# Issue order planned from other operation costs, LayerNorm squares on ScalarE, and a norm's squares summed on VectorE

## Chip, cores and metric

The kernel runs on one core of one Trainium2 chip. The metric is the device time of one execution in microseconds (us). The core's engines are TensorE (PE in the rows, its weight loads PEld), VectorE (DVE, V in the code), ScalarE (ACT, S), GpSimd (POOL, G) and SyncE (SP, Q), which issues nearly all DMA transfers.

## What is computed

One block of an encoder on 512 tokens with 1024 channels, all in float32. `rms_norm` divides by the root of the mean square over the channels.

```python
x = x + 0.5 * swiglu_ffn(rms_norm(x, ffn1_norm[l]), ffn1_w13[l], ffn1_w2[l])
h = rms_norm(x, mix_norm[l])
proj = h @ w_in[l]
a, g, q, k, v, fl = jnp.split(proj, splits, axis=-1)
y_conv = conv_module(a, g, conv_w[l], conv_b[l], conv_ln_g[l], conv_ln_b[l])
y_attn = forgetting_attention(q, k, v, fl + forget_b[l])
y = jnp.concatenate([rms_norm(y_conv, out_norm_conv[l]),
                     rms_norm(y_attn, out_norm_attn[l])], axis=-1)
x = x + y @ w_out[l]
x = x + 0.5 * swiglu_ffn(rms_norm(x, ffn2_norm[l]), ffn2_w13[l], ffn2_w2[l])
...
return rms_norm(x, final_norm)
```

`conv_module` is a gated input, a causal depthwise convolution of 31 taps over 512 channels, LayerNorm over those channels, and silu. `forgetting_attention` is causal softmax attention of 8 heads of 64, with a bias from a running sum of log-sigmoid gates. Each half-step (`swiglu_ffn`) has 2816 hidden channels.

## The kernel before

Channels lie on the 128 partitions and the 512 tokens along the free axis, so x is 8 tiles of 128x512. A product of full precision is made from three passes: each operand is split into a high part in the reduced format fp32r and a low rest, and high·high, high·low and low·high are summed in one PSUM bank. So a product over 1024 channels is 24 matmuls of 512 columns. The activations' parts are `xh` and `xl`. A weight tile (`raw`, 512 KB by DMA) gets its high part `whi` by a ScalarE copy and its low part `wlo` by a VectorE subtraction; each has two buffers (`SPLITS`), which are taken in the order of the weight units: `whi81` for the first attention pair's q, `whi82` for its k, `whi83` and `whi84` for the second pair's, up to `whi88`, then `whi89` for the output projection.

The stages are: the first half-step (products `f1g`, `f1u`, `f1p`, `f1o`); the input projection, which gives the convolution's gate and value (`pg`, `pa`), values and gates of attention (`pv`), and q and k of four pairs of heads (`pq`, `pk`); convolution and attention beside these; the output projection (`wo`, part 0 from the convolution's channels, part 1 from the attention's); and the second half-step (`f2g`, `f2u`, `f2p`, `f2o`) with the final norm.

The four tiles of the convolution (`conv_tile`) are summed tap by tap: tiles 1 and 3 on VectorE (`conv`), tiles 0 and 2 by a ScalarE product per tap (`tap`, two buffers) and a GpSimd addition (`acc`). Attention (`attention`) goes per pair of heads, block of 128 queries and head: scores `s` on PE into one of two banks, a VectorE instruction that adds the gate's bias and takes the minimum (`sm`, `mn`), an exponential on ScalarE, a transposition on PE (`pt`, one bank), a ScalarE copy (`pT`), and the product with the values (`po`). `pt5_0` and `s5_3` are such steps of head 5, blocks 0 and 3.

After the last tap LayerNorm is made in `conv_norm`: the mean by a PE sum over the partitions (`ssq_mean`) that is spread back (`rb_mean`), VectorE subtracts it from the four tiles, GpSimd squares them (`sq_ln`), PE sums the squares (`ssq_ln`), ScalarE takes the root (`rc_ln`), VectorE the reciprocal, PE spreads it (`rb_ln`), ScalarE copies it (`rstd_ln`), and then the tiles are scaled, put through silu and split into `yh` and `yl`. Their squares (`sq_conv`) go to PE for a further norm (`ssq_conv`, `rb_conv`).

The class `Stats` sums squares in one of two ways: `pair` gives two squared tiles at a time to PE, and `add` has VectorE add each square to an accumulator, which PE sums once, in `rstd`. For the second half-step's norm (`f2in`) the kernel before uses `pair` in `w_out`, part 1. The first `f2g` product doesn't need that norm; its result is scaled by `rstd_f2in` when it leaves PSUM. Products share three PSUM banks (`mm`).

ScalarE holds one table of functions at a time. Root, sigmoid, exponential and silu each ask for an `ACT_TABLE_LOAD` if another table is loaded.

The order of all instructions is set by `Plan`. The code records operations with their engine and the tiles that they read and write; `price` gives each a cost, and `schedule` places them one by one: the operation that can start earliest on its engine, and among those the one with the highest rank, which is the longest path of costs behind it plus an urgency (`URGENT...`, given where it is recorded). A change of the ScalarE table costs 1.3 in this plan and lowers the rank by 40. All recorded instructions show as line 240 in the profile, so the rows are told apart by tile names.

Of the kernel before, what the change touches and what calls it, by code (L numbers as in the profile page):

```python
# [36 lines left out]
P = 128  # L37
T = 512
D = 1024
KD = D // P  # L40
# [33 lines left out]
SEM = 0.15  # L74
COPY, ACT = 0.05, 0.07
PENALTY = 40.0
URGENT_IN, URGENT_STATS, URGENT_V, URGENT_LF, URGENT_LN, URGENT_END = 20.0, 200.0, 200.0, 200.0, 200.0, 200.0
URGENT_Q, URGENT_OUT, URGENT, URGENT_X = 3.0, 3.0, 50.0, 50.0

# [65 lines left out]
class Buf:  # L145
    def __init__(self, make, dt, slots):
        self.make, self.dt, self.slots, self.tile = make, dt, slots, None
        self.uses, self.left = [], 0

# [15 lines left out]
class Plan:  # L165
# [5 lines left out]
    def __init__(self, tc):  # L171
        self.tc, self.ops, self.tags, self.joined, self.urgency = tc, [], {}, None, 0.0

    def tile(self, pool, shape, dt, tag, name, bufs=1):
        slots = self.tags.setdefault((id(pool), tag), Slots(bufs))
        buf = Buf(lambda: pool.tile(shape, dt, tag=tag, name=name, bufs=bufs), dt, slots)
        slots.queue.append(buf)
        size = int(np.prod(shape))
        if View._bytes.size < size:
# [64 lines left out]
    def price(self, engine, method, args, kwargs, out):  # L244

        n = out.n if isinstance(out, View) else 512
        if engine == "PE":
            dt = args[1].buf.dt
            passes = 4 if dt == F32 and method == "matmul" else 2 if dt == F32 else 1
            part = args[1].at[0].size / P if method == "matmul" else 1  # L250
            return 0.003 + n * passes / 2400.0 * max(part, 0.25), None
        if method == "dma_start" and engine != "Q":
            return 0.1, None
        if engine == "S":
            if method == "copy":
                return COPY + n * 0.00084, None
            return ACT + n * 0.00084, None if args[2] in (AF.Copy, AF.Square, AF.Identity) else args[2]
        if engine == "G":
            return 0.1 + n * (0.0024 if method.startswith("tensor_") else 0.0012), None
        if engine == "Q":  # L260
            return 0.1 + n * 4 * P / 330e3, None
        if method == "tensor_tensor_scan":
            return 0.06 + n * 0.0022, None
        if method == "reciprocal":
            return 0.06 + n * 0.0064, None
        if method == "scalar_tensor_tensor":
            return 0.06 + n * 0.00118, None
        return 0.06 + n * 0.00108, None

# [96 lines left out]
def block_kernel(ctx: ExitStack, tc, x_d, w13a, w2a, wag, wvf, wqk, wo, w13b, w2b, par_d, out_d):  # L366
# [5 lines left out]
    sb = ctx.enter_context(tc.tile_pool(name="sb", bufs=1))  # L372
    pp = ctx.enter_context(tc.tile_pool(name="pp", bufs=1, space=bass.MemoryType.PSUM))
    dr = ctx.enter_context(tc.tile_pool(name="dr", bufs=1, space=bass.MemoryType.DRAM))

# [123 lines left out]
    class Stats:  # L499
# [6 lines left out]

        def square(self, src, engine=S):
            sq = tile_([P, T], self.tag, f"sq_{self.name}{self.i}", BUFS[self.tag])[:, :NT * self.w]
            with plan.urgent(URGENT_STATS):
                if engine is S:  # L510
# [5 lines left out]

        def add(self, src, engine=V):

# [3 lines left out]
            else:  # L522
                sq = self.square(src)
                with plan.urgent(URGENT_STATS):
                    engine.tensor_add(self.acc, self.acc, sq)
# [562 lines left out]
    def conv_norm():  # L1088
# [7 lines left out]
        for i in range(NC):  # L1096
            V.tensor_sub(conv[i], conv[i], pm)
            ln.pair(ln.square(conv[i], G), i == NC - 1)
        lr = ln.rstd()
# [10 lines left out]
    def w_out(part, d, w, r):  # L1110
# [9 lines left out]
        if part == 1:  # L1120
            split_x(d, G_FFN2)
            st2.pair(st2.square(xs[d]), d == KD - 1)

# [78 lines left out]
```

## Time and profile before

| | us |
|---|---|
| median of 3 runs (lowest, highest) | 947.99 (947.40, 948.77) |
| the profiled execution | 948.41 |
| its span in the trace | 946.7 |

The span is 1.7 us shorter than the execution's own time: that lies around the first and the last instruction. TensorE's mean granted clock is 0.996 of full speed. In the rows, a time is the start from the span's beginning, then the duration; matmuls overlap, so the distance between two starts, not the duration, tells how long PE is held. What stands in square brackets is the idle time of the engine before that row and what ended it.

### The profile page before, as it was taken

The numbers are of one execution on the slowest core, as the hardware profiler recorded it, in microseconds if no ns is written. First come the engines' busy times: TensorE is split into PE (matmuls) and PEld (weight loads), VectorE is DVE, ScalarE is ACT, GpSimd is POOL, SyncE is SP. The second block draws the span as 40 slices with busy tenths as digits, with TensorE's granted clock in tenths as the row PEclk, the third lists the DMA queues.
The fourth block names the chain that finished last, engine by engine and source line by source line (L and its number), as shares of the span: only waits on it lengthen the run. The fifth ranks groups of instructions, "written<-read, shape, count | busy, mean of one in ns | idle before, by whom it ended". The sixth has DMA issues, their size and how long they took to land.

```text
span 946.7 us, 13399 instructions
## 1 busy us (share of the span) xinstructions
PE 932.5 (99%) x5261; PEld 793.8 (84%) x5261; DVE 650.1 (69%) x983; ACT 430.5 (45%) x670; POOL 154.0 (16%) x132
## 2 busy tenths in 40 slices
PE   9999999999999999999999999999999999999996
PEld 7888999988999888898676777888898988999886
DVE  6655887657767465898977776555877755867554
ACT  7433433334333245676869655333433333333252
POOL 1000211001111000999842000000121001111000
PEclk9999999999999999999999999999999999999998
DMA  7222323222432132323212112223332222323122
GB/s 254 84 89 97 126 95 107 77 101 73 144 118 85 51 111 90 95 86 115 87 68 65 48 67 90 89 91 110 113 111 89 89 90 89 134 93 114 61 68 89
DMA packets 33135, 91.19 MB, mean 96 GB/s; under 512 B 3496, under 2 KB 12840, under 8 KB 33072
## 3 DMA queue, kind: packets, MB, share of 16 engines
q1 hardware_dynamic: 32528, 89.94, 28.1%
q8 instruction: 41, 0.67, 0.3%
q10 hardware_dynamic: 544, 0.40, 0.1%
q14 instruction: 22, 0.18, 0.1%
HBM read 88.21 MB, written 2.11 MB: 95 GB/s over the span
## 4 chain that ended last, share of the span: by engine, by line
PE 89%; DVE 3%; POOL 3%; ACT 3%; issue 1%; DMA 1%; SPq 0%; DVEq 0%; POOLq 0%
PE f2g L240 13%; PE f2u L240 13%; PE f1u L240 13%; PE f1g L240 13%; PE f1p L240 9%; PE f2p L240 9%; PE wo L240 5%; PE f2o L240 4%; PE f1o L240 3%; POOL acc L240 3%; PE pg L240 1%; PE pq L240 1%; PE pa L240 1%; PE s L240 1%; PE po L240 1%
## 5 line engine op out<-in xcount | busy, mean ns | idle before, releaser
L240 ACT CAST whi<-raw 128x1024 fp32r<-128x1024 f32 (+3 forms) x153 | 151.5, 990 | 291.1 <-issue 135.9
L240 DVE TENSOR_TENSOR wlo<-raw,whi 128x1024 fp32r<-128x1024 f32 (+3 forms) x153 | 185.7, 1213 | 21.6 <-ACT whi L240 18.9
L240 POOL TENSOR_TENSOR acc<-acc,tap 128x512 f32<-128x512 f32 x60 | 90.0, 1500 | 81.1 <-ACT tap L240 74.5
L240 PE MATMUL f1u<-xh,whi 128*128 128x512 f32 x176 | 68.8, 391 | 0.5 <-ACT xh L240 0.5
L240 PE MATMUL f1u<-xl,whi 128*128 128x512 f32 x176 | 68.6, 390 | 0.3 <-DVE xl L240 0.3
L240 PE MATMUL f2g<-xh,whi 128*128 128x512 f32 x176 | 68.7, 390 | 0.0
L240 PE MATMUL f2g<-xl,whi 128*128 128x512 f32 x176 | 68.6, 390 | 0.0
L240 PE MATMUL f2u<-xh,whi 128*128 128x512 f32 x176 | 68.6, 390 | 0.0
L240 PE MATMUL f1u<-xh,wlo 128*128 128x512 f32 x176 | 68.5, 389 | 0.0
L240 PE MATMUL f2u<-xl,whi 128*128 128x512 f32 x176 | 68.5, 389 | 0.0
L240 PE MATMUL f2g<-xh,wlo 128*128 128x512 f32 x176 | 68.5, 389 | 0.0
L240 PE MATMUL f2u<-xh,wlo 128*128 128x512 f32 x176 | 68.5, 389 | 0.0
L240 PE MATMUL f1g<-xh,whi 128*128 128x512 f32 x168 | 65.9, 392 | 0.0
L240 PE MATMUL f1g<-xl,whi 128*128 128x512 f32 x168 | 65.7, 391 | 0.0
L240 PE MATMUL f1g<-xh,wlo 128*128 128x512 f32 x168 | 65.4, 389 | 0.0
L240 POOL TENSOR_TENSOR f2S<-raw 128x512 f32<-128x512 f32 x8 | 11.1, 1386 | 310.6 <-DMA raw<-w2b 294.0
L240 DVE TENSOR_TENSOR f2un<-f2u,rstd_f2in 128x512 f32<-128x512 f32 x22 | 15.2, 690 | 61.8 <-PE f2u L240 61.8
L240 POOL TENSOR_TENSOR f1S<-raw 128x512 f32<-128x512 f32 x8 | 10.4, 1295 | 260.3 <-DMA raw<-w2a 224.2
L240 ACT ACTIVATE tap<-u,par 128x512 f32<-128x512 f32 x60 | 42.8, 720 | 21.0 <-POOL acc L240 20.7
L240 DVE TENSOR_TENSOR f1un<-f1u,rstd_in 128x512 f32<-128x512 f32 x22 | 15.2, 689 | 53.6 <-PE f1u L240 53.6
L240 DVE SCALAR_TENSOR_TENSOR conv<-u,par,conv 128x512 f32<-128x512 f32 x60 | 45.1, 752 | 1.2
L240 PEld LDWEIGHTS f1u<-xh,whi 128*128 128x128 f32 x176 | 33.0, 188 | 8.0 <-ACT xh L240 0.9
(409 smaller groups left out, 2401.1 us busy)
## 6 DMA issues: line engine op xcount, KB each, us to landing
raw<-w13b SPq DMA_DIRECT2D x44, 512.0 KB, 3.5
raw<-w13a SPq DMA_DIRECT2D x42, 512.0 KB, 3.5
raw<-w2a SPq DMA_DIRECT2D x16, 512.0 KB, 3.6
raw<-w2b SPq DMA_DIRECT2D x16, 512.0 KB, 3.5
raw<-wag SPq DMA_DIRECT2D x8, 512.0 KB, 3.5
raw<-wqk SPq DMA_DIRECT2D x8, 512.0 KB, 3.6
raw<-wo SPq DMA_DIRECT2D x8, 512.0 KB, 3.5
raw<-w2a SPq DMA_DIRECT2D x16, 192.0 KB, 2.4
```

Of the source, the lines that this page charges most:

```text
L240: ins = getattr(target, method)(*real, **kw)
```

## The change

It has three parts. First, `price` gives other costs: they now depend on whether a PSUM tile is an operand (a new flag on each buffer), VectorE operations without one get a factor `SHARED`, and the urgency of attention (`URGENT`) goes from 50 to 80. No operation is added by this part, but the order that `schedule` makes changes on all engines. Second, `conv_norm` squares the LayerNorm tiles on ScalarE and not on GpSimd. Third, in part 1 of `w_out` the squares for the second half-step's norm are added up by VectorE, all but the last, with urgency 0; PE then sums the accumulator and the last square. Names and table switches are as before, and so are the DMA transfers' count and sizes.

```diff
-COPY, ACT = 0.05, 0.07
+SHARED = 1.15
...
-URGENT_Q, URGENT_OUT, URGENT, URGENT_X = 3.0, 3.0, 50.0, 50.0
+URGENT_Q, URGENT_OUT, URGENT, URGENT_X = 3.0, 3.0, 80.0, 50.0
...
         if engine == "PE":
-            dt = args[1].buf.dt
-            passes = 4 if dt == F32 and method == "matmul" else 2 if dt == F32 else 1
-            part = args[1].at[0].size / P if method == "matmul" else 1
-            return 0.003 + n * passes / 2400.0 * max(part, 0.25), None
+            if method != "matmul":
+                return n * 0.00084, None
+            part = args[1].at[0].size / P
+            if args[1].buf.dt != F32:
+                return 0.0133 + n / 2400.0, None
+            if part > 0.5:
+                return 2 * max(0.02 + n * 0.00069, 0.1), None
+            return (0.13 if part > 0.3 else 0.084) * max(n, 64) / P, None
...
         if engine == "S":
+            cost = (0.143 if psum else 0.2) + n * 0.00084 - 0.05
             if method == "copy":
-                return COPY + n * 0.00084, None
...
-        return 0.06 + n * 0.00108, None
...
+        if not psum:
+            cost *= SHARED
+        return 0.1 + cost, None
...
-        def square(self, src, engine=S):
+        def square(self, src, engine=S, by=URGENT_STATS):
...
-            with plan.urgent(URGENT_STATS):
+            with plan.urgent(by):
...
-                sq = self.square(src)
-                with plan.urgent(URGENT_STATS):
+                sq = self.square(src, by=by)
+                with plan.urgent(by):
                     engine.tensor_add(self.acc, self.acc, sq)
...
-            ln.pair(ln.square(conv[i], G), i == NC - 1)
+            ln.pair(ln.square(conv[i]), i == NC - 1)
...
-            st2.pair(st2.square(xs[d]), d == KD - 1)
+            if d < KD - 1:
+                st2.add(xs[d], by=0.0)
+            else:
+                st2.wait = [st2.square(xs[d])]
```

The new order at three places. In each listing a row is one instruction, output first, then inputs, then the shape; the numbers behind the names tell buffers apart and differ between the two programs.

PE at the first scores of attention, before: all 24 matmuls of the second pair's q (`pq`, weights `whi83`) stand ahead of them, and the second pair's k (`pk`) behind.

```order
L240 MATMUL pq_4066<-xh_193,wlo_4033 128x512
L240 MATMUL pq_4066<-xh_207,whi_4019 128x512
L240 MATMUL pq_4066<-xl_214,whi_4019 128x512
L240 MATMUL pq_4066<-xh_207,wlo_4033 128x512
L240 MATMUL s_0_4117<-k_4075,q_2778 128x128
L240 LDWEIGHTS ident_103
L240 MATMUL s_0_4117<-mask_84,ident_103 128x128
L240 MATMUL s_0_4122<-k_4075,q_2799 128x128
L240 LDWEIGHTS ident_103
L240 MATMUL s_0_4122<-mask_84,ident_103 128x128
L240 MATMUL pk_4126<-xh_106,whi_4071 128x512
```

The same place now: the scores stand behind the first 9 matmuls of that product.

```order
L241 MATMUL pq_4062<-xh_136,whi_4009 128x512
L241 MATMUL pq_4062<-xl_144,whi_4009 128x512
L241 MATMUL pq_4062<-xh_136,wlo_4026 128x512
L241 MATMUL s_0_4084<-k_4074,q_2778 128x128
L241 LDWEIGHTS ident_102
L241 MATMUL s_0_4084<-mask_86,ident_102 128x128
L241 MATMUL s_0_4087<-k_4074,q_2799 128x128
L241 LDWEIGHTS ident_102
L241 MATMUL s_0_4087<-mask_86,ident_102 128x128
L241 MATMUL pq_4062<-xh_150,whi_4009 128x512
L241 MATMUL pq_4062<-xl_158,whi_4009 128x512
```

The scores moved ahead by 15 product matmuls; their k (`k_4074`) is written by VectorE, behind the running sum of the gates (`cum`), a `wlo`, three additions to the convolution's tile 3 and the two halves of q. In VectorE's rows before, from `cum` on:

```order
L240 SCALAR_TENSOR_TENSOR q_2778<-pq_3959,rstd_f1n 64x512
L240 SCALAR_TENSOR_TENSOR cum<-one,pc 8x512
L240 TENSOR_TENSOR wlo_4033<-raw_3903,whi_4019 128x1024
L240 SCALAR_TENSOR_TENSOR conv_3988<-u_2871,par,conv_3988 128x512
L240 SCALAR_TENSOR_TENSOR q_2799<-pq_3959,rstd_f1n 64x512
L240 SCALAR_TENSOR_TENSOR conv_3988<-u_2871,par,conv_3988 128x512 x2
L240 TENSOR_TENSOR k_4075<-pk_4015,rstd_f1n 128x512
```

and now:

```order
L241 SCALAR_TENSOR_TENSOR cum<-one,pc 8x512
L241 TENSOR_TENSOR wlo_4026<-raw_3894,whi_4009 128x1024
L241 SCALAR_TENSOR_TENSOR conv_3982<-u_2871,par,conv_3982 128x512
L241 SCALAR_TENSOR_TENSOR q_2778<-pq_3955,rstd_f1n 64x512
L241 SCALAR_TENSOR_TENSOR conv_3982<-u_2871,par,conv_3982 128x512
L241 SCALAR_TENSOR_TENSOR q_2799<-pq_3955,rstd_f1n 64x512
L241 SCALAR_TENSOR_TENSOR conv_3982<-u_2871,par,conv_3982 128x512
L241 TENSOR_TENSOR k_4074<-pk_4011,rstd_f1n 128x512
```

The running sum and that `wlo` moved ahead of the first half of q; the rest keeps its order. On ScalarE two taps fewer now stand ahead of the `whi` that this `wlo` waits for.

ScalarE around the silu of the convolution, before: the fourth exponential here (`sm_0_4685`, head 5, block 0) and the cast of the output projection's first weights (`whi_4721`) stand ahead of the load of silu's table.

```order
L240 ACTIVATE sm_0_4685,sums_4694<-sm_0_4685,mn_0_4686 128x128
L240 CAST whi_4721<-raw_4302 128x1024
L240 COPY rstd_ln<-rb_ln 128x512
L240 COPY pT_0_4743<-pt_0_4727 128x128
L240 ACTIVATE sm_2_4733,sums_4694<-sm_2_4733,mn_2_4734 128x384
L240 CAST q_4746<-qn_4717 64x512
L240 CAST q_4752<-qn_4717 64x512
L240 COPY pT_0_4762<-pt_0_4754 128x128
L240 ACT_TABLE_LOAD
L240 ACTIVATE acc_3363<-acc_3363,par 128x512
```

The same place now:

```order
L241 ACTIVATE sm_2_4727,sums_4695<-sm_2_4727,mn_2_4728 128x384
L241 ACT_TABLE_LOAD
L241 ACTIVATE acc_3363<-acc_3363,par 128x512
L241 ACTIVATE acc_3931<-acc_3931,par 128x512
L241 ACTIVATE yh_4763<-acc_3363,par 128x512
L241 ACTIVATE yh_4768<-acc_3931,par 128x512
...
L241 COPY pT_0_4802<-pt_0_4716 128x128
L241 ACT_TABLE_LOAD
L241 ACTIVATE sm_0_4683,sums_4695<-sm_0_4683,mn_0_4684 128x128
L241 CAST whi_4809<-raw_4342 128x1024
```

That exponential and that cast now stand behind the whole silu block (four silu, four `yh`) and another table load. PE's rows that wait for them, now: the transposition `pt_0_4811` of that exponential stands between the two halves of `ssq_conv`, ahead of everything of the output projection.

```order
L241 MATMUL pk_4721<-xh_206,wlo_4554 128x512
L241 MATMUL ssq_conv<-sq_conv_4758,ones 32x128 x4
L241 MATMUL ssq_conv<-sq_conv_4772,ones 32x128 x4
L241 MATMUL pt_0_4811<-ident,sm_0_4683 128x128
L241 MATMUL ssq_conv<-sq_conv_4796,ones 32x128 x4
L241 MATMUL ssq_conv<-sq_conv_4807,ones 32x128 x4
L241 MATMUL s_3_4828<-k_4573,q_4527 128x512
```

In the kernel before, that transposition stood inside the product `pk`, and the first `ssq_conv` behind the first matmuls of `wo`. For the third part the order shows one group of `ssq_f2in` matmuls on PE inside the second `f2g` product, where there were four, three of them inside `wo` products and one in the first `f2g`; `rb_f2in` follows 12 product matmuls later, and 6 product matmuls after it the second `f2u` product starts.

## Rows read from the trace of the kernel before

**Rows 1.** Part 1 of the page: busy time, share of the span and instructions of each engine.

```profile
PE 932.5 (99%) x5261; PEld 793.8 (84%) x5261; DVE 650.1 (69%) x983; ACT 430.5 (45%) x670; POOL 154.0 (16%) x132
```

**Rows 2.** Windows of 25 us: the window and its length, then busy time (instructions) of PE, PEld, DVE, ACT and POOL, the granted clock of TensorE, the share of the DMA engines, GB/s.

```profile
450.00:475.00 25.00, 22.65 (x146) 15.96 (x145) 22.71 (x46) 20.98 (x46) 19.89 (x16) 1.00 0.22 79
500.00:525.00 25.00, 24.20 (x171) 18.12 (x170) 20.49 (x35) 24.39 (x47) 8.24 (x8) 1.00 0.21 66
575.00:600.00 25.00, 25.00 (x141) 20.05 (x140) 14.31 (x19) 11.32 (x16) 0.00 (x0) 1.00 0.27 85
```

**Rows 3.** PE's timeline from the convolution's last product to the first pair's scores.

```profile
425.15 0.39 PE L240 MATMUL pa<-xl,whi 128*128 128x512 f32 x1
426.12 0.50 PE L240 MATMUL pa<-xh,wlo 128*128 128x512 f32 x1 [0.59 <-DVE wlo L240]
...
442.85 0.39 PE L240 MATMUL pq<-xl,whi 128*128 128x512 f32 x1
443.32 0.50 PE L240 MATMUL pq<-xh,wlo 128*128 128x512 f32 x1
443.66 0.39 PE L240 MATMUL pq<-xh,whi 128*128 128x512 f32 x1
...
448.22 0.39 PE L240 MATMUL pq<-xh,wlo 128*128 128x512 f32 x1
...
450.27 0.40 PE L240 MATMUL pk<-xh,wlo 128*128 128x512 f32 x1
452.14 0.70 PE L240 MATMUL s<-k,q 128*128 128x256 f32 x2 [1.47 <-DVE mn L240]
...
453.78 0.40 PE L240 MATMUL pk<-xh,wlo 128*128 128x512 f32 x1
454.93 0.91 PE L240 MATMUL s<-k,q 128*128 128x384 f32 x2 [0.75 <-DVE mn L240]
```

**Rows 4.** VectorE's timeline from the running sum of the gates to the first pair's k.

```profile
439.16 1.20 DVE L240 TENSOR_TENSOR_SCAN cum<-one,pc 8x512 f32<-8x512 f32 x1
441.17 2.10 DVE L240 TENSOR_TENSOR wlo<-raw,whi 128x1024 fp32r<-128x1024 f32 x1 [0.81 <-ACT whi L240]
443.19 0.74 DVE L240 SCALAR_TENSOR_TENSOR conv<-u,par,conv 128x512 f32<-128x512 f32 x1
...
446.27 0.69 DVE L240 TENSOR_TENSOR k<-pk,rstd_f1n 128x512 f32<-128x512 f32 x1
```

**Rows 5.** GpSimd's timeline at the squares of LayerNorm.

```profile
489.03 2.04 POOL L240 TENSOR_TENSOR sq_ln<-acc 128x512 f32<-128x512 f32 x2 [5.28 <-DVE acc L240]
...
493.02 2.81 POOL L240 TENSOR_TENSOR sq_ln<-acc 128x512 f32<-128x512 f32 x2
```

**Rows 6.** PE's timeline from the second sum of LayerNorm's squares to the first output products.

```profile
498.34 0.64 PE L240 MATMUL ssq_ln<-sq_ln,ones 128*32 128x128 f32 x16
...
511.09 0.40 PE L240 MATMUL wo<-yh,whi 128*128 128x512 f32 x1
511.72 0.50 PE L240 MATMUL wo<-yl,whi 128*128 128x512 f32 x1 [0.24 <-DVE yl L240]
...
513.55 0.40 PE L240 MATMUL wo<-yh,wlo 128*128 128x512 f32 x1
514.41 0.44 PE L240 MATMUL pt<-ident,sm 128*128 128x128 f32 x2 [0.46 <-ACT pT L240]
```

**Rows 7.** ScalarE's timeline up to the silu block.

```profile
503.29 0.39 ACT L240 ACTIVATE sm<-sm,mn 128x128 f32<-128x128 f32 x1
...
503.67 1.03 ACT L240 CAST whi<-raw 128x1024 fp32r<-128x1024 f32 x1
...
505.85 1.25 ACT L240 CAST q<-qn 64x512 fp32r<-64x512 f32 x2
...
507.41 1.28 ACT L240 ACT_TABLE_LOAD   x1
508.71 1.52 ACT L240 ACTIVATE acc<-acc,par 128x512 f32<-128x512 f32 x2
510.14 1.32 ACT L240 ACTIVATE yh<-acc,par 128x512 fp32r<-128x512 f32 x2
```

**Rows 8.** PE's timeline at the first of the four sums of the second half-step's squares, then the groups of instructions: the squares themselves, all eight (busy us, mean ns of one, idle time before them).

```profile
564.41 0.39 PE L240 MATMUL wo<-yh,wlo 128*128 128x512 f32 x1
564.74 0.64 PE L240 MATMUL ssq_f2in<-sq_f2in,ones 128*32 128x128 f32 x16
565.31 0.51 PE L240 MATMUL wo<-yh,whi 128*128 128x512 f32 x1
565.65 0.40 PE L240 MATMUL wo<-yl,whi 128*128 128x512 f32 x1
...
L240 ACT ACTIVATE sq_f2in<-x 128x512 f32<-128x512 f32 x8 | 5.1, 633 | 10.7 <-DVE x L240 10.7
```

**Rows 9.** Timeline of PE, ScalarE and VectorE where the second half-step's norm is spread and first used.

```profile
585.00 1.05 PE L240 MATMUL rb_f2in<-rc_f2in,sel 128*128 128x128 f32 x8
585.81 0.48 PE L240 MATMUL f2u<-xh,whi 128*128 128x512 f32 x1
...
586.09 0.59 ACT L240 COPY rstd_f2in<-rb_f2in 128x512 f32<-128x512 f32 x1
...
587.18 0.68 DVE L240 TENSOR_TENSOR f2gn<-f2g,rstd_f2in 128x512 f32<-128x512 f32 x1
```

More of the change, by code (lines that the diff above doesn't have):

```diff
@@ L147, in __init__ @@
         self.make, self.dt, self.slots, self.tile = make, dt, slots, None
-        self.uses, self.left = [], 0
+        self.uses, self.left, self.psum = [], 0, False
 class Slots:
@@ L171, in __init__ @@
     def __init__(self, tc):
-        self.tc, self.ops, self.tags, self.joined, self.urgency = tc, [], {}, None, 0.0
+        self.tc, self.ops, self.tags, self.joined, self.urgency, self.psum = tc, [], {}, None, 0.0, None
     def tile(self, pool, shape, dt, tag, name, bufs=1):
@@ L177, in tile @@
         slots.queue.append(buf)
+        buf.psum = pool is self.psum
         size = int(np.prod(shape))
@@ L247, in price @@
         if engine == "PE":
-            dt = args[1].buf.dt
-            passes = 4 if dt == F32 and method == "matmul" else 2 if dt == F32 else 1
-            part = args[1].at[0].size / P if method == "matmul" else 1
-            return 0.003 + n * passes / 2400.0 * max(part, 0.25), None
+            if method != "matmul":
[6 more added lines that the diff above has]
+            return (0.13 if part > 0.3 else 0.084) * max(n, 64) / P, None
         if method == "dma_start" and engine != "Q":
             return 0.1, None
+        psum = any(isinstance(v, View) and v.buf.psum for v in list(args) + list(kwargs.values()))
         if engine == "S":
+            cost = (0.143 if psum else 0.2) + n * 0.00084 - 0.05
             if method == "copy":
-                return COPY + n * 0.00084, None
-            return ACT + n * 0.00084, None if args[2] in (AF.Copy, AF.Square, AF.Identity) else args[2]
+                return cost, None
+            if isinstance(kwargs.get("scale"), View) or isinstance(kwargs.get("bias"), View):
+                cost += 0.09
+            return (cost + (0.19 if "accum_out" in kwargs else 0.0),
+                    None if args[2] in (AF.Copy, AF.Square, AF.Identity) else args[2])
         if engine == "G":
-            return 0.1 + n * (0.0024 if method.startswith("tensor_") else 0.0012), None
+            return 0.1 + n * (0.0026 if method.startswith("tensor_") else 0.0009), None
         if engine == "Q":
@@ L264, in price @@
         if method == "reciprocal":
-            return 0.06 + n * 0.0064, None
+            return 0.1 + n * 0.0062, None
         if method == "scalar_tensor_tensor":
-            return 0.06 + n * 0.00118, None
-        return 0.06 + n * 0.00108, None
+            cost = n * 0.00118
+        elif method in ("tensor_copy", "tensor_scalar") and not psum:
+            cost = n * 0.0006
+        else:
+            cost = n * 0.00105
+        if not psum:
+            cost *= SHARED
+        return 0.1 + cost, None
     def schedule(self):
@@ L373, in block_kernel @@
     pp = ctx.enter_context(tc.tile_pool(name="pp", bufs=1, space=bass.MemoryType.PSUM))
+    plan.psum = pp
     dr = ctx.enter_context(tc.tile_pool(name="dr", bufs=1, space=bass.MemoryType.DRAM))
@@ L515, in square, with add @@
             return sq
-        def add(self, src, engine=V):
+        def add(self, src, engine=V, by=URGENT_STATS):
             if self.acc is None:
@@ L1121, in w_out @@
             split_x(d, G_FFN2)
-            st2.pair(st2.square(xs[d]), d == KD - 1)
+            if d < KD - 1:
+                st2.add(xs[d], by=0.0)
+            else:
+                st2.wait = [st2.square(xs[d])]
     st2 = Stats("f2in", D)
```

## The prediction

> **What bounds the kernel now.** The busy shares come first: PE is busy 932.5 of 946.7 us, VectorE 650, ScalarE 430 [rows 1]. A kernel like this gets faster in two ways only: PE gets less work, or PE's idle time shrinks. The windows tell where there is idle time: PE is busy in all 25 us of 575 to 600, but only in 22.65 of 450 to 475 and 24.20 of 500 to 525 [rows 2]. That is the stretch of convolution and attention, where VectorE has 22.71 and ScalarE 20.98 to 24.39 busy us of 25, so the order in which these two serve PE decides there. The price of a product matmul is read from 20 of them without a stop: 443.66 to 448.22, 0.228 us each [rows 3]. A start that comes later than that after the one before is PE time lost.
>
> By that measure the large losses are these. In the convolution's last product 425.15 to 426.12 loses 0.74, for a `wlo`. In the second pair's q 442.85 to 443.32 loses 0.24. At the first pair's scores 450.27 to 452.14 loses 1.64 and 453.78 to 454.93 loses 0.92: PE waits for VectorE's `mn`, as the score banks are not read in time [rows 3]. At the first output products 511.09 to 511.72 loses 0.40 (`yl`) and 513.55 to 514.41 loses 0.63 (a transposition waits for a `pT` copy) [rows 6]. Together 4.57 us, the most that a better order could give back there.
>
> **Third part: the squares for the second half-step.** One group of `ssq_f2in` on PE stands at 564.74 between product matmuls that start at 564.41 and 565.31 [rows 8]. From 564.41 to 565.65 it is 1.24 us for what would be two pitches, 0.456, so a group costs PE 0.78, in a stretch where PE has no idle time that could absorb it [rows 2]. Four groups become one: 3 x 0.78 = **2.35 us removed**, all on the path. What is added is six additions of 128x512 on VectorE. A VectorE operation of that form takes 0.69 (the k at 446.27 [rows 4]), so 4.1 us; VectorE is busy 14.31 of 25 there [rows 2], and by the order they stand behind the work that PE needs. I cost them at nothing; without that cover they would delay a `wlo` by up to 0.69 each. The ScalarE squares stay (eight of 0.633 [rows 8]). The sum is now known later: it stands in the second `f2g`, and the second `f2u` needs the PSUM bank of the first `f2g`, which comes free when `f2gn` has read it. After `rb_f2in` come 6 product matmuls, 1.37, with some 0.1 at their start. After the same `rb_f2in`, whose end I put at the next product's start 585.81, the copy to `rstd_f2in` starts 0.28 later and takes 0.59, and `f2gn` takes 0.68 [rows 9]: 1.55, and some 0.1 between the two engines. So PE would wait **about 0.2**, with bounds 0 and 0.6 (an addition or a `wlo` of VectorE ahead).
>
> **First part: the new order at the first scores.** PE reaches the first scores after 9 matmuls of the second pair's q and not after 24. Before, its second matmul started at 442.85, so the first at 442.62. The 0.74 at `pa` goes, since that `wlo` is now made earlier on VectorE, and about 0.35 comes back at the first pair's q for the next `wlo` (an estimate; bounds 0 and 0.74). PE is then at the scores at 442.62 - 0.39 + 9 x 0.228 = 444.3. They need k. On VectorE the running sum no longer stands behind half of q, so it starts at about 438.6, not 439.16, and ends at 439.7. The `wlo` behind it waited 0.81 for its `whi` [rows 4]; two taps fewer stand ahead of that `whi`, so I let it start at once and take its 2.10: 441.8. Three convolution additions of 0.74 [rows 4] and two halves of q, at 0.69 like the k, follow: 445.4, and k ends at 446.1 to 446.2. So **a new wait of about 1.9** stands at the first scores; bounds 0.6 (if all of VectorE comes 1.3 earlier) and 3.2 (if the `whi` is no earlier than before). In exchange the scores start 4 us earlier and spread, so that 1.64, 0.92 and 0.24 should go. Balance of this place: -0.74 - 0.24 - 1.64 - 0.92 + 0.35 + 1.9 = **-1.3**.
>
> **Second part with the first: LayerNorm and the silu block.** GpSimd's squares ran from 489.03 to 495.83 [rows 5]. On ScalarE a square takes 0.633 [rows 8], so four are 2.5 instead of 4.85 busy us, and GpSimd's casts no longer stand between them. The second `ssq_ln` on PE starts at 498.34 [rows 6]. By the new order PE has less ahead of it (it follows `rb_mean` by six product matmuls and the steps of two heads); counted with the same durations it ends at about 495.6 and not 498.9, 3.3 earlier. From there silu took 508.71 - 498.9 = 9.8. In that stretch ScalarE also ran the cast of `whi` (1.03) and the two q casts (1.25) [rows 7], which now stand elsewhere, so I take 7.6 and let silu start at 503.2. The block of four silu and four `yh` is twice 1.43 (from 508.71 to 510.14) and 1.32, so 5.5; then come one short copy, a table load of 1.28 and an exponential of 0.39 [rows 7]: the exponential of head 5 ends at **about 510.8**.
>
> PE waits for just that. The old order had PE at `wo` at 511.09. The new order has moved one score group and two or three transpositions, about 1.2 us, from ahead of this point to behind it, puts the first half of `ssq_conv` (0.57) ahead, and PE comes 1.3 earlier by the place above: 511.09 - 1.2 + 0.57 - 1.3 = 509.2, or up to 0.9 earlier if small gaps in between go too; I take 508.6. So **a new wait of about 2.2** at `pt5_0`; bounds 0 (LayerNorm 2 us sooner than walked) and 7 (no sooner than before). Behind it the cast of `whi`, its `wlo` and the next `pT` (behind another table load, the root of `ssq_conv`) take their place as waits of `wo`: about 0.8, where the old ones, 0.40 and 0.63, go. Balance of this place: +2.2 + 0.8 - 1.03 = **+2.0**.
>
> A table load here takes 1.28, and the silu behind it starts 0.02 after the load ends [rows 7]. The Trainium skill, "ScalarE: Activation LUTs", section "What ACT_TABLE_LOAD costs", puts a switch at about 2.66 us, 1.28 for the load and 1.38 for a drain, and its rules ask to do all of one set before switching, which speaks against an exponential moved behind silu. By that price the two loads in the chain to `pt5_0` would make it 2.8 longer, and the sum below would come out at +1.3 and the time at 949.3; the rows show no such drain, so they decide.
>
> **Sum.** -2.35 + 0.2 - 1.3 + 2.0 = **-1.45**; the head, the tail and all other products keep their instructions. Against the profiled execution that is 948.41 - 1.45 = 946.96. That execution is 0.42 above the median, so on the median 947.99 the forecast is 946.5.
>
> **Rivals.** (a) *The plan keeps its word*: with costs nearer to those of the trace, the new order was placed without these two waits, and in the run VectorE and ScalarE are there in time. For it speaks that both waits are differences of long walks; against it that both chains are rows in fixed order. Without them the sum is -1.45 - 4.1 = -5.5, so 942.4; with half of them 944.5. (b) *Slower: the exponential behind silu.* If LayerNorm's chain does not come sooner, since it hangs on VectorE's last tap and PE's place for `ssq_mean` (now behind the whole of a `pk` product) and not on GpSimd's squares, the silu block starts at 508.7 as before. The exponential then ends 5.5 later, and all of it is PE's wait: -1.45 + 5.5 = +4.0, so 952.0. It makes the kernel slower by more than the measurement's grain as soon as the chain comes 3.4 us later than I walked it. (c) *The third part doesn't pay*: PE loses three groups, but waits for the later `rstd_f2in`, behind ScalarE's casts and VectorE's additions. If `f2gn` comes 2 us later than walked, the sum is +0.55: 948.5.
>
> **How the numbers follow.** A measurement of this kernel can tell about 0.2% from no change, so below 946.1 is faster and above 949.9 slower. My forecast's own range is 945.0 to 948.0, from the bounds of the two waits taken half; chance 0.47, of which about 0.13 lies below 946.1. (a) 0.30, (b) 0.18, (c) 0.05, nearly all of it no change. So faster 0.43, same 0.39, slower 0.18. For 8 in 10 the range reaches down to 942.6, just above the full case (a), and up to 950.2, a little less than half of the way that (b) adds.
>
> **What would show it.** Right: one `ssq_f2in` group on PE and 575 to 600 still full; no loss of over 0.5 at the second and third score blocks, but one idle row of 1 to 3 us ahead of the first `s` that waits for DVE k, and one ahead of a `pt` that waits for ACT, near 508 to 511; silu about 5 us earlier. The forecast is wrong if PE's idle time from 425 to 525 shrinks to under 1 us, which is (a), if silu starts no sooner than 507, which is (b), or if PE stops at the second `f2u` for over 1 us, which is (c).

## The result, and the profile after

The change makes the kernel slower by a little: a median of 949.76 us in 21 runs (949.03 to 951.68), against 948.63 us in 21 runs of the kernel before (947.40 to 949.50). The ratio, taken over all runs and not of the two medians, is 1.0017, with a 95% interval of 1.0011 to 1.0023, so about 1.6 us; the medians are 1.1 apart, since nine of the changed kernel's times lie well above the rest. One execution of one experiment, the exponential ahead of silu, took 3287.56 us and is left out of its ratio. The forecast was 946.5, that is 1.5 us faster. The profiled execution took 949.4 us with a span of 947.7; before these were 948.41 and 946.7.

The page's first part, to hold against [rows 1]:

```profile
PE 931.5 (98%) x5213; PEld 793.4 (84%) x5213; DVE 654.2 (69%) x989; ACT 433.6 (46%) x674; POOL 148.0 (16%) x128
```

PE has 48 instructions fewer, as three sums of squares left it, and its busy time falls by only 1.0 us although their own cost was 2.35. Some PE work must have become slower. The windows of 25 us show where (columns as in [rows 2]). The kernel before, in the two windows of this stretch that [rows 2] leaves out:

```profile
425.00:450.00 25.00, 24.33 (x111) 19.46 (x110) 22.09 (x38) 17.62 (x25) 23.00 (x16) 1.00 0.34 113
475.00:500.00 25.00, 24.87 (x216) 17.89 (x214) 18.75 (x35) 16.99 (x37) 10.00 (x9) 1.00 0.18 64
```

The changed kernel:

```profile
425.00:450.00 25.00, 22.45 (x102) 17.20 (x100) 21.86 (x39) 17.00 (x24) 20.95 (x15) 1.00 0.31 107
450.00:475.00 25.00, 25.00 (x172) 17.75 (x172) 22.49 (x48) 20.63 (x49) 15.49 (x12) 1.00 0.25 85
475.00:500.00 25.00, 25.00 (x202) 18.56 (x201) 19.51 (x34) 19.61 (x38) 11.82 (x10) 1.00 0.19 64
500.00:525.00 25.00, 22.11 (x142) 16.91 (x141) 18.31 (x33) 23.86 (x45) 7.93 (x8) 0.93 0.13 44
```

The order did what it was planned for in the middle: PE's 2.35 idle us at 450 to 475 [rows 2] are gone. But 2.55 idle us stand ahead of them now, against 0.67, and 2.89 at 500 to 525, against 0.80. Over the 100 us PE's idle time went from 3.95 to 5.44 us. And the last window has what no window of the kernel before had here: a granted clock of 0.93.

They are the two waits that the prediction named, one for k and one for the exponential. PE's timeline at the first pair's q, where a `wlo` is late, and at both:

```profile
431.52 0.39 PE L241 MATMUL pq<-xl,whi 128*128 128x512 f32 x1
432.21 0.50 PE L241 MATMUL pq<-xh,wlo 128*128 128x512 f32 x1 [0.30 <-DVE wlo L241]
...
445.08 0.39 PE L241 MATMUL pq<-xh,wlo 128*128 128x512 f32 x1
447.72 0.46 PE L241 MATMUL s<-k,q 128*128 128x128 f32 x2 [2.25 <-DVE k L241]
...
510.33 0.65 PE L241 MATMUL ssq_conv<-sq_conv,ones 128*32 128x128 f32 x16
513.86 0.33 PE L241 MATMUL pt<-ident,sm 128*128 128x128 f32 x1 [2.89 <-ACT sm L241]
...
516.09 0.78 PE L241 MATMUL wo<-yh,whi 128*128 128x512 f32 x1
516.66 0.63 PE L241 MATMUL wo<-yl,whi 128*128 128x512 f32 x1
```

A `wo` matmul lasts 0.63 to 0.78 here and 0.40 to 0.50 in [rows 6]. The windows of 2 us behind the second wait say why; the granted clock is the first number behind the busy times:

```profile
511.00:513.00 2.00, 0.00 (x0) 0.00 (x0) 2.00 (x3) 2.00 (x4) 1.92 (x3) 1.00 0.00 0
513.00:515.00 2.00, 1.14 (x18) 0.61 (x19) 1.25 (x4) 1.97 (x6) 1.90 (x2) 1.00 0.00 0
515.00:517.00 2.00, 2.00 (x7) 1.37 (x8) 1.53 (x2) 1.97 (x4) 0.00 (x0) 0.53 0.00 0
517.00:519.00 2.00, 2.00 (x8) 1.53 (x7) 1.74 (x5) 1.99 (x4) 0.00 (x0) 0.62 0.86 272
```

PE stood still from 511 to 513.9, worked at the full clock for one more us, and then the clock stood at its lower level, 1.2 GHz, until about 518.3. The mean of 0.93 over 25 us is 1.75 us of full-speed time lost. The Trainium skill, "TensorE: Matmul & The Clock Gate", section "HAM oscillation — how this bites in real kernels", describes that a wait of PE can put the clock back to the lower level, so that the work behind the wait starts slow; the rows agree, but for that one us at the full clock first.

ScalarE at the same place shows the chain that PE waits for:

```profile
506.48 1.52 ACT L241 ACTIVATE acc<-acc,par 128x512 f32<-128x512 f32 x2
...
512.02 1.28 ACT L241 ACT_TABLE_LOAD   x1
513.32 0.40 ACT L241 ACTIVATE sm<-sm,mn 128x128 f32<-128x128 f32 x1
```

Silu comes at 506.48 and not at 508.71 [rows 7], 2.2 us sooner, and the exponential of head 5 stands behind the whole silu block and a table load. The load takes 1.28 and the exponential starts 0.02 after it. So the 1.38 us of drain that the Trainium skill's "ScalarE: Activation LUTs", section "What ACT_TABLE_LOAD costs", adds to a switch doesn't show here either. The 949.3 that this price would have given lies near the measured 949.76 by chance.

The walk had put silu at 503.2. What is missing is the gain of LayerNorm's squares. PE's rows of that chain, one of the kernel before and two of the changed kernel:

```profile
485.62 0.64 PE L240 MATMUL ssq_mean<-acc,mean 128*32 128x128 f32 x16
```

```profile
488.72 0.65 PE L241 MATMUL ssq_mean<-acc,mean 128*32 128x128 f32 x16
...
498.07 0.64 PE L241 MATMUL ssq_ln<-sq_ln,ones 128*32 128x128 f32 x16
```

The new order has the second `ssq_mean` behind a whole `pk` product, 3.1 us later, and that uses up what the squares on ScalarE save: the second `ssq_ln` starts 0.3 us sooner than in [rows 6], not 3.3. From its end to silu it is 7.8 us, about the 7.6 that were forecast, for 9.8 before. So nearly all of the 2.2 us comes from that last stretch, where the two casts no longer stand.

The second half-step, PE and VectorE, to hold against [rows 9]:

```profile
595.28 1.06 PE L241 MATMUL rb_f2in<-rc_f2in,sel 128*128 128x128 f32 x8
...
597.00 0.69 DVE L241 TENSOR_TENSOR f2gn<-f2g,rstd_f2in 128x512 f32<-128x512 f32 x1 [3.03 <-ACT rstd_f2in L241]
...
597.74 0.50 PE L241 MATMUL f2u<-xh,whi 128*128 128x512 f32 x1
```

From `rb_f2in` to the second `f2u` it is 2.46 us. The 0.8 of `rb_f2in` itself (585.00 to 585.81 in [rows 9]) and six product matmuls with their start, 1.47, leave 0.2 of waiting, as forecast.

For the profiled execution the books close: 1.5 more idle us, 1.75 by the clock, 2.35 less work and 0.2 for the bank give +1.1, and it is 1.0 longer.

### The profile page after: what moved, and what is told of

Its sections match the earlier page's. It is cut to its first block, busy times and chain, and to the rows that moved or that the text cites. A ratio compares the mean times of both kernels' runs of the same rounds, so it can differ in the third digit from the quotient of the medians.

```text
span 947.7 us, 13285 instructions
## 1 busy us (share of the span) xinstructions
PE 931.5 (98%) x5213; PEld 793.4 (84%) x5213; DVE 654.2 (69%) x989; ACT 433.6 (46%) x674; POOL 148.0 (16%) x128
## 4 chain that ended last, share of the span: by engine, by line
PE 90%; DVE 5%; ACT 2%; issue 1%; DMA 1%; POOL 0%; SPq 0%; DVEq 0%; POOLq 0%
PE f2g L241 13%; PE f2u L241 13%; PE f1u L241 13%; PE f1g L241 13%; PE f1p L241 9%; PE f2p L241 9%; PE wo L241 5%; PE f2o L241 4%; PE f1o L241 3%; DVE conv L241 2%; PE s L241 2%; PE pq L241 2%; PE pk L241 1%; PE pg L241 1%; PE pa L241 1%; PE po L241 1%
```

## The experiments

All ratios are against the kernel before, with their 95% intervals; the changed kernel itself has 1.0017 (1.0011 to 1.0023).

### The third part alone

```diff
 # the kernel before
-            st2.pair(st2.square(xs[d]), d == KD - 1)
+            if d < KD - 1:
+                st2.add(xs[d], by=0.0)
+            else:
+                st2.wait = [st2.square(xs[d])]
```

Expected:

> The kernel before with the third part alone: squares for the second half-step's norm summed by VectorE, old costs and urgency. The order changes there only. Theory A: three groups of 0.78 us leave PE and a wait of 0.2 for the bank of the first f2g comes in: 2.0 to 2.2 us faster than the kernel before (ratio 0.9977). Rival: the later norm makes PE wait or delays wlo casts by as much: within 0.5 us of the kernel before.

Measured: 946.26 us, ratio 0.9977 (0.9968 to 0.9986), 2.2 us faster (1.3 to 3.0). The term was -2.35 + 0.2. The 0.2 is not seen in this order: the last group stands inside an `f2u` product here, `rb_f2in` starts at 587.70 and the next `f2u` matmul at 588.51, which is its own 0.8 and no wait.

### The changed kernel without the third part

```diff
 # the changed kernel
-            if d < KD - 1:
-                st2.add(xs[d], by=0.0)
-            else:
-                st2.wait = [st2.square(xs[d])]
+            st2.pair(st2.square(xs[d]), d == KD - 1)
```

> The changed kernel without its third part: the squares of the second half-step go to PE in pairs again; new costs, new urgency and LayerNorm's squares on ScalarE stay. Theory A: the parts add up, since the third part lies behind the stretch of attention: 2.1 to 2.4 us slower than the changed kernel, so some 3.5 us slower than the kernel before (952, ratio 1.0037). Rival: in the changed kernel the third part is worth less, since PE waits for the later norm there: under 1 us slower than the changed kernel.

Measured: 951.98 us, ratio 1.0040 (1.0028 to 1.0053), 2.2 us slower than the changed kernel. The third part is worth the same in both, within the intervals, so the first two parts together cost 3.8 us.

### The first part alone, and the second part alone

```diff
 # the changed kernel without the third part
-            ln.pair(ln.square(conv[i]), i == NC - 1)
+            ln.pair(ln.square(conv[i], G), i == NC - 1)
```

> The kernel before with the first part alone: new costs and urgency in the planner, LayerNorm's squares on GpSimd, squares of the second half-step to PE in pairs. Theory A: the new order is what loses, by the wait for k at the first scores and the place of silu among ScalarE's exponentials: 2 to 5 us slower than the kernel before (951 to 954). Rival: the order is sound and it is the squares on ScalarE, which fill up that engine, that lose: within 1 us of the kernel before.

Measured: 953.07 us, ratio 1.0049 (1.0037 to 1.0062), 4.6 us slower, as theory A said. The second `ssq_ln` starts at 501.68 here, 3.3 us later than in the kernel before [rows 6]: with the squares still on GpSimd, the later `ssq_mean` (488.40) shows in full. The same wait for k stands at the first scores. At `wo` PE waits 1.20 us for a `yh` and 0.62 for a `yl`, and the clock falls there too. PE's rows and two windows:

```profile
512.96 0.50 PE L241 MATMUL wo<-yh,whi 128*128 128x512 f32 x1 [1.20 <-ACT yh L241]
514.08 0.79 PE L241 MATMUL wo<-yl,whi 128*128 128x512 f32 x1 [0.62 <-DVE yl L241]
```

```profile
512.00:514.00 2.00, 0.50 (x1) 0.19 (x1) 1.64 (x3) 2.00 (x4) 2.00 (x2) 1.00 0.31 119
514.00:516.00 2.00, 1.92 (x18) 1.10 (x18) 2.00 (x4) 2.00 (x4) 1.33 (x2) 0.50 0.69 266
```

```diff
 # the kernel before
-            ln.pair(ln.square(conv[i], G), i == NC - 1)
+            ln.pair(ln.square(conv[i]), i == NC - 1)
```

> The kernel before with the second part alone: LayerNorm's squares on ScalarE under the old costs. The planner's order changes from there on. Theory A: LayerNorm's chain comes 1 to 3 us earlier, but PE is bound there by other work: within 1.2 us of the kernel before, either way. Rival: ScalarE, which is busy 24.4 of 25 us at 500 to 525, pays for 2.5 us more work and PE waits for it: 1.5 to 3 us slower than the kernel before.

Measured: 949.54 us, ratio 1.0011 (1.0003 to 1.0020), 1.0 us slower, within theory A's 1.2. With `ssq_mean` where it was, the squares on ScalarE bring the second `ssq_ln` forward by 3.6 us, to 494.77 from 498.34 [rows 6], and silu by 4.3, to 504.39 from 508.71 [rows 7]. PE gets nothing of it: the output projection's first `wlo` is not there. PE at LayerNorm's sum, then ScalarE, then PE, then a window:

```profile
494.77 0.65 PE L240 MATMUL ssq_ln<-sq_ln,ones 128*32 128x128 f32 x16
```

```profile
504.39 1.52 ACT L240 ACTIVATE acc<-acc,par 128x512 f32<-128x512 f32 x2
```

```profile
511.46 0.39 PE L240 MATMUL wo<-yl,whi 128*128 128x512 f32 x1
513.43 0.50 PE L240 MATMUL wo<-yh,wlo 128*128 128x512 f32 x1 [1.58 <-DVE wlo L240]
```

```profile
516.00:518.00 2.00, 2.00 (x7) 1.52 (x6) 1.96 (x4) 1.97 (x4) 0.00 (x0) 0.50 0.05 21
```

The two waits of the kernel before at this place, 0.40 and 0.63 [rows 6], have become one of 1.75, and behind it the clock falls.

### Is it the idle time or the clock? Matmuls in the waits

15 matmuls of 384 columns, into columns that nobody reads, run while PE would wait for the exponential. They compute nothing of the result.

```diff
 # the changed kernel; emitted ahead of pt5_0
+            for _ in range(15):
+                ins = nc.tensor.matmul(stats.ps[:, P:].ap(), xh[0][:, :P].ap(), xh[1][:, P:].ap(), start=False, stop=False)
+                ...
```

> The changed kernel, with 15 matmuls of 384 columns on PE ahead of pt5_0, into columns of a PSUM bank that nobody reads; they run while PE would wait for the exponential, some 2.6 of the 2.9 us. Theory A: the wait itself stays, but PE is not idle in it, so the granted clock stays at 1.00 and the work from 515 to 518.3 takes half of its 3.3 us: 1.5 to 1.7 us faster than the changed kernel, about as fast as the kernel before (within 0.5 us). Theory B: the clock's fall does not follow from the idle time, or what runs at half clock waits for ScalarE and VectorE anyway: no gain, within 0.4 us of the changed kernel.

Measured: 948.53 us, ratio 1.0002 (0.9993 to 1.0011), 1.4 us faster than the changed kernel by the ratios, with more work on PE; the two intervals only touch, at 1.0011. The transposition still waits for the same exponential, and the clock stays up. PE, then a window:

```profile
511.32 2.88 PE L1138 MATMUL ssq_conv<-xh,xh 128*128 128x384 f32 x15
514.28 0.33 PE L244 MATMUL pt<-ident,sm 128*128 128x128 f32 x1
...
516.05 0.48 PE L244 MATMUL wo<-yh,whi 128*128 128x512 f32 x1
```

```profile
516.00:518.00 2.00, 1.69 (x11) 1.15 (x9) 2.00 (x5) 1.97 (x4) 0.00 (x0) 1.00 0.22 53
```

So the fall of the clock is a cost of its own, beside the wait, and PE's standing still brings it.

A second run fills the wait at the first scores as well:

```diff
 # the run above; emitted ahead of s0_0
+                        for n in range(12):
+                            ins = nc.tensor.matmul(first[:, P:].ap(), xh[0][:, :P].ap(), xh[1][:, P:].ap(),
+                                                   start=n == 0, stop=n == 11)
+                            ...
```

> The changed kernel with idle matmuls on PE in both waits: 15 of 384 columns ahead of pt5_0, as in the run before, and 12 ahead of the first scores, into columns that nobody reads. Theory A: in some executions the granted clock falls to 0.50 behind the wait for k too (a profile of a variant shows it from 447.7 to 450.5, where the changed kernel's shows 1.00), and that is what splits the changed kernel's times into 949.0 to 949.9 and 950.2 to 951.7. With PE busy in both waits the times stay together within 1.5 us, and the median is 0.2 to 0.6 below the run with one filler, so 948.0 to 948.3. Rival: the spread has another cause: the same median and the same spread as with one filler (948.5, 947.9 to 949.5).

Measured: 948.16 us, ratio 0.9999 (0.9990 to 1.0008), and the times lie within 1.24 us (947.77 to 949.01). The changed kernel's 21 times are 12 from 949.0 to 949.9 and 9 from 950.2 to 951.7. The mean granted clock of the executions tells what sets the 9 apart: it is 0.9946 on average in the 12 and 0.9929 in the 9, and 0.0017 of 948 us is 1.6 us, for the 1.5 between the means of their times. With the second wait filled, the 3 slowest of 11 executions have 0.994 or 0.995 and 7 of the other 8 have 0.996 or 0.997; with both filled, all 11 have 0.996 or 0.997. None of the 9 was traced, but the next run's profile shows such a fall at the first wait, with the same order there: the changed kernel and that run, in turn.

```profile
449.00:451.00 2.00, 2.00 (x10) 1.28 (x9) 1.97 (x7) 1.97 (x3) 1.92 (x2) 1.00 0.09 20
```

```profile
449.00:451.00 2.00, 2.00 (x7) 1.61 (x6) 1.97 (x7) 1.97 (x4) 1.92 (x2) 0.51 0.19 39
```

After the same wait of 2.4 us the clock falls in one execution and not in another.

### The exponential ahead of silu

```diff
 # the changed kernel, ScalarE's order; "..." is the silu block
+ACTIVATE sm5_0
+COPY pT4_0
 ACT_TABLE_LOAD
 ...
-COPY pT4_0
-ACT_TABLE_LOAD
-ACTIVATE sm5_0
```

> The changed kernel, with two ScalarE operations moved ahead of the load of silu's table: the copy pT4_0 and the exponential of head 5, block 0; one table load falls away by that. Everything else keeps its order. Theory A: PE's idle 2.9 us ahead of pt5_0, and TensorE's half clock (granted 0.50) for some 3 us after it, come from that exponential standing behind the silu block. Without it wo can start when its weights are there, about 513 instead of 516.1, at full clock: 2.5 to 4 us faster than the changed kernel, so 1 to 2.5 us faster than the kernel before (946 to 947.5). Theory B: PE's idle time is set by what comes next anyway (the cast of wo's weights behind the same silu block), so the wait moves to wo and the clock falls there too: less than 1.3 us, the table load's price, against the changed kernel.

Measured: 950.67 us, ratio 1.0021 (1.0012 to 1.0030), no faster than the changed kernel. Theory B had the direction right, with another step than it named: the transposition runs at once, and PE waits for the squares of the silu tiles on GpSimd, which now start later. Behind these waits the clock falls too, to 0.50 from 516 to 519. PE's rows:

```profile
511.87 0.33 PE L244 MATMUL pt<-ident,sm 128*128 128x128 f32 x1
514.50 0.43 PE L244 MATMUL ssq_conv<-sq_conv,ones 128*32 128x128 f32 x8 [2.30 <-POOL sq_conv L244]
515.95 0.65 PE L244 MATMUL ssq_conv<-sq_conv,ones 128*32 128x128 f32 x8 [1.02 <-POOL sq_conv L244]
```

### The first scores later

```diff
 # the changed kernel, PE's order
+MATMUL pq1 (the 15 matmuls that were behind)
 MATMUL s0_0, s1_0
-MATMUL pq1 (15, among later scores)
```

> The changed kernel, with the 15 matmuls of the second pair's q that stand behind the first scores put ahead of them on PE, as in the kernel before. Theory A: they fill PE's 2.2 to 2.4 us of waiting for k at 445 to 447.7, and nothing of it is given back: 1.5 to 2.4 us faster than the changed kernel. Rival: the early scores are what makes the later scores flow; with the scores 3.4 us later PE waits at the second and third blocks again (1.64 and 0.92 in the kernel before): within 0.7 us of the changed kernel.

Measured: 949.01 us, ratio 1.0008 (0.9999 to 1.0017), about 0.8 us faster than the changed kernel, if at all (the intervals overlap), and not 1.5 to 2.4, so nearer to the rival's "within 0.7". The wait for k is gone, and waits for `mn` are back:

```profile
PE s L244 <- DVE mn L244: 1.2, 2, 0.7
```

### Costs or urgency

```diff
 # first run: the changed kernel
-URGENT_Q, URGENT_OUT, URGENT, URGENT_X = 3.0, 3.0, 80.0, 50.0
+URGENT_Q, URGENT_OUT, URGENT, URGENT_X = 3.0, 3.0, 50.0, 50.0
 # second run: the kernel before
-URGENT_Q, URGENT_OUT, URGENT, URGENT_X = 3.0, 3.0, 50.0, 50.0
+URGENT_Q, URGENT_OUT, URGENT, URGENT_X = 3.0, 3.0, 80.0, 50.0
```

> The changed kernel with the urgency of attention left at 50: new costs, squares on ScalarE and sums on VectorE stay. In its order the exponentials of the third pair's heads all stand behind the silu block. Theory A: any order in which PE stops for over 1.5 us near the first output products loses the wait and, with the clock at 0.50 behind it, half of it again; new costs with urgency 50 are no better at that: 949 to 953. Rival: it is the urgency alone that spoiled the order, and the new costs are worth something without it: under 946.5.

> The kernel before with the urgency of attention at 80 and nothing else. Theory A: the new costs and not the urgency bring the waits: within 2 us of the kernel before. Rival: the urgency brings them: 2 to 5 us slower, as the first part alone is.

Measured: 951.37 us, ratio 1.0028 (1.0018 to 1.0039), and 949.94 us, ratio 1.0012 (1.0003 to 1.0021). Both are slower than the kernel before, so both rivals are refuted: the new costs are not worth something without the urgency, and the urgency alone does not lose 2 to 5 us. The urgency alone is enough to bring the wait for k at the first scores, with the old costs:

```profile
PE s L240 <- DVE k L240: 1.9, 1, 1.9
```

The clock stays at 1.00 there, and PE's idle time from 425 to 475 is the same as before, 3.04 for 3.02 us. Where this run loses its 1.2 us was not found: from 400 to 550 PE is idle for 4.2 us, for 4.0 before.

With the new costs and urgency 50 the wait for k is not there. PE stops at the second score blocks instead, and the clock falls there. PE, then windows:

```profile
453.27 0.80 PE L241 MATMUL s<-k,q 128*128 128x256 f32 x1 [2.74 <-DVE mn L241]
```

```profile
453.00:453.50 0.50, 0.23 (x1) 0.23 (x2) 0.50 (x6) 0.48 (x2) 0.50 (x1) 0.50 0.04 16
454.00:456.00 2.00, 2.00 (x7) 1.26 (x6) 1.46 (x4) 1.99 (x5) 1.17 (x2) 0.50 0.00 0
```

Theory A of this run had the size right, but named the first output products as the place; there PE lost only 0.45 us at most in one piece. The wait for the exponential is in neither run.

### Two attempts to mend

The first takes the kernel before with the second and third part, and moves the weights that the second part alone had waited for:

```diff
 # old costs, second and third part; order of ScalarE and VectorE
+CAST whi89
 ACTIVATE acc2 (silu)
 ...
-CAST whi89
+TENSOR_TENSOR wlo89
 SCALAR_TENSOR_TENSOR yl2
 ...
-TENSOR_TENSOR wlo89
```

> The kernel before with the second and third part under the old costs and urgency, and the cast and subtraction for the first weights of the output projection (whi89, wlo89) moved ahead of the second silu pair on ScalarE and of the second pair of yl on VectorE. With the second part alone PE stopped there for 1.6 us for that wlo, and the clock stood at 0.50 for 3.3 us behind it. Theory A: the squares on ScalarE gain their 4 us for silu, and that gain is lost only at these weights; with them early the wait and the clock's fall go: 947.2 (second and third parts added to the kernel before) less 1.6, less 1.6 for the clock, plus up to 1 for a silu pair that comes later: 944 to 945.5, faster than the third part alone (946.3). Rival: the wait moves on to the second half of ssq_conv or to yl, and the clock falls there: 946.5 to 948.

Measured: 946.89 us, ratio 0.9981 (0.9973 to 0.9990). The wait for the `wlo` is gone and the clock stays at 1.00, but PE now stops for 0.91 at the next transposition. That is the rival's time without its fall of the clock, and no better than the third part alone:

```profile
513.24 0.40 PE L243 MATMUL wo<-yh,wlo 128*128 128x512 f32 x1
514.39 0.33 PE L243 MATMUL pt<-ident,sm 128*128 128x128 f32 x1 [0.75 <-ACT sm L243]
```

The second takes the changed kernel and moves everything that had been named:

```diff
 # the changed kernel, order
 PE: +pq1 ahead of s0_0; +pt5_0 inside pk3; +ssq_conv (second half) behind wo01's first three;
     +rb_conv behind wo02's first three
 ACT: +pT4_0, sm5_0 ahead of silu's table; +pT5_0, whi89 ahead of the second silu pair
 DVE: +wlo89 ahead of yl2
```

> The changed kernel with all named waits attacked: the second pair's q ahead of the first scores; pT4_0 and the exponential of head 5 ahead of silu's table load; pt5_0 inside pk; its copy and the cast whi89 between the two silu pairs, wlo89 ahead of the second pair of yl; the second half of ssq_conv behind the first matmuls of the second wo product and rb_conv behind the first of the third. Theory A: PE has no wait over 1.2 us in 440 to 525 and keeps its full clock: 945 to 947, 3 to 4.5 us faster than the changed kernel. Rival: the chain from silu to the output products is the limit in this order, whichever step stands next to it; a wait of 2 us or more stays and the clock falls: 948.5 or more.

Measured: 957.28 us, ratio 1.0090 (1.0075 to 1.0106), a failure, as the rival said. A score block on PE waits 5.37 us for VectorE's `mn`, which stands behind the `wlo` and the second pair of `yl`, and the `wo` matmuls behind it last 0.63 to 0.78 again. PE, then VectorE:

```profile
515.53 1.19 PE L244 MATMUL s<-k,q 128*128 128x512 f32 x2 [5.37 <-DVE mn L244]
```

```profile
510.81 1.21 DVE L244 TENSOR_TENSOR wlo<-raw,whi 128x1024 fp32r<-128x1024 f32 x1
512.00 2.91 DVE L244 SCALAR_TENSOR_TENSOR yl<-acc,par,yh 128x512 fp32r<-128x512 f32 x2
514.83 0.55 DVE L244 CUSTOM_DVE_ANT_0 sm<-s,ck 128x384 f32<-128x384 f32 x1
```

The same two steps in the trace of the changed kernel, GpSimd and VectorE:

```profile
511.40 2.98 POOL L241 TENSOR_TENSOR sq_conv<-acc 128x512 f32<-128x512 f32 x2
```

```profile
514.23 0.56 DVE L241 CUSTOM_DVE_ANT_0 sm<-s,ck 128x384 f32<-128x384 f32 x1 [0.75 <-PE pt L241]
```

So three chains end near each other in the changed order: the exponential at 513.7, GpSimd's squares at 514.4 and this `mn` at 514.8, 0.75 of it a wait for that transposition. Taking away one shows the next.

## Why the prediction was wrong

The time, 949.76, lies outside the forecast's own range of 945.0 to 948.0 and inside the one for 8 in 10, 942.6 to 950.2. The sign was wrong: the forecast was a gain of 1.5 us, less than the 0.2% that the prediction itself calls no change, and it is a loss of 1.6.

The third part was right in mechanism and size: -2.35 + 0.2 forecast, -2.2 measured, in the kernel before and in the changed one; the small wait of 0.2 shows in the changed kernel only.

The step that failed is the balance of the silu place, "+2.0". What the term lacked is the clock. A wait of this size was priced as its length alone, and behind it TensorE ran for some 3.3 us at 1.2 GHz: 1.75 us in the profile, and 1.4 us by the ratios of the changed kernel and the run with the filled wait. That alone turns the forecast's sign.

Its idle time came out right, but by luck: from 475 to 525 PE's idle time grew from 0.93 to 2.89 us, by 1.96. The exponential ended at 513.7 and not 510.8, since LayerNorm's sum came 0.3 us sooner and not 3.3. PE was there at 510.9 and not 508.6, so the wait was 2.9 and not 2.2. And the 0.8 of waits at `wo` behind it did not come: at the lower clock PE has no idle time there. In the run with the filled wait 0.48 of it is back, for a `pT`, which may be why that run gains 1.4 and not 1.75. Two walks that are wrong by about as much, and a term that was hidden, left the sum where it was forecast.

The balance of the first scores, "-1.3", was too good by about 0.8: from 425 to 475 PE's idle time went from 3.02 to 2.55 us, by -0.5. The wait for k came as named, at 2.2 to 2.4 for 1.9, again with both of its ends later than walked: k was ready at 447.6 and not 446.2, and PE was there at 445.3 and not 444.3. With its own wait the prediction's scores start 2.2 us sooner than before, and not the 4 that it says; they started 0.7 sooner, and the later waits were gone all the same. The wait at `pa` went too, but a wait of the same kind came back at the first q, 0.46 by the changed kernel's distances for the 0.35 assumed, and smaller ones ahead of it. In some executions the clock falls behind this wait as well; the executions' mean clocks, and the times of the run with both waits filled, which stay together, speak for that as the reason for the spread.

With the measured sizes the same sum gives -2.15 - 0.5 + 2.0 + 1.75 = +1.1 for the profiled execution, which was 1.0 longer.

Rival (a) is refuted: both waits are there. Rival (b) had the right place and sign, and its condition held for LayerNorm's sum: with `ssq_mean` behind the `pk` product that it names, the sum came only 0.3 us sooner. But silu did come sooner, by 2.2 us, as casts went elsewhere; (b)'s own sign, silu no sooner than 507, was missed by 0.5. That the chain does not hang on GpSimd's squares at all is refuted: alone, their move to ScalarE brings silu forward by 4.3 us, though PE gains nothing and the time is 1.0 us longer. Rival (c) is refuted by the third part alone. The upper end of the range for 8 in 10, 950.2, was called a little less than half of the way that (b) adds; from 946.5 to 952.0 it is two thirds.

What stays open: how much of the 4.6 us of the first part alone belongs to which cost in `price`. Costs and urgency were only taken apart as a whole. The run with the new costs and urgency 50 has the second and third parts too, so these runs don't tell whether the two add up; each order has its own waits.

## What to carry to other kernels

Price a wait of the engine that bounds the kernel with what it does to the clock: where the clock fell, behind 1.75, 1.8 (in two pieces), 2.9 and 3.0 us without work, the mean clock of those 25 us was 0.93 each time, so 1.75 us were lost on top, whatever the length; in the kernel before idle time in pieces of at most 1.6 us left it at 1.00. When a chain is made faster, name the two or three chains that end right behind it, because they take its place, as GpSimd's squares and a `mn` did here; and look for where the new order puts the step ahead of it, as with `ssq_mean`. A change that takes work off the full engine without touching the tight stretch is worth its own cost: the third part alone, at 0.9977, beats both kernels, and nothing tried with it was measurably better.

## What the runs showed of the hardware that was not expected

The same wait of 2.4 us at the first scores left the granted clock at 1.00 in the profile of the changed kernel and brought it to 0.51 in that of the kernel with the early exponential. At `wo`, waits of 1.75 us, and of 1.20 and 0.62 in a row, were followed by a clock of 0.50, while a wait of 1.9 us for k, with the urgency alone, left it at 1.00. The length of the wait alone doesn't tell whether the clock falls. Nor is the moment the same: in the changed kernel PE worked for about a us at 1.00 behind the wait before it fell, and with the new costs and urgency 50 it stood at 0.50 from 453.0 on, before the first matmul behind the wait at 453.27.
